# A mixture-of-experts stage: one branch for each whole product, with the folds inside the short way

## The chip, the cores and the metric

One core of a Trainium2 chip runs the whole program. The metric is the device time of one execution in microseconds (us), median of the runs. Engines are named as in the profile: PE is TensorE (matmul), PEld its weight loads, DVE is VectorE, ACT is ScalarE, POOL is GpSimd, SP issues DMAs.

## What is computed

Two layers of a hybrid decoder over 256 tokens of width 1024, in float32. The change touches only the channel mixer of the second layer, eight SwiGLU experts of which each token takes two:

```python
def moe_swiglu(x, w_router, w_gate, w_up, w_down):
    ...
    for e in range(N_EXPERTS):
        y = y + gates[:, e:e + 1] * swiglu(xt, w_gate[e], w_up[e], w_down[e])
    ...
# swiglu: (silu(x @ w_gate) * (x @ w_up)) @ w_down; 1024 -> 3584 -> 1024 for each expert
```

## The kernel before

Float32 products are made of three matmuls in a rounded format: each operand is split into a high part and a low rest, and hi·hi + hi·lo + lo·hi are added up (`mm3`, lines 161 to 164). A split of a weight tile (128 x 1024) is a cast on ScalarE (`whi`, line 152) and a subtraction on VectorE (`wlo`, line 153). Both kinds of tile have five buffers (`SPL`).

The tokens of an expert are gathered into up to 128 rows (`xg`, high and low side by side); 3584 is cut into seven pieces of 512, `m`. **A stage** is one pair (e, m). It makes gate(e, m), 4 splits; then `turn` transposes the hidden tile `hh` of the stage before into `ht` (four transposes, line 167, then ACT writes its high half, line 922, and DVE its low half, line 924); then up(e, m), 4 splits; then down of the stage before, 4 splits. So a stage has 12 splits, numbered here from 0: gate 0 to 3, up 4 to 7, down 8 to 11. Weights come in by chunks of two splits (1 MB) over SP's queue, some twelve chunks ahead.

**Two ways.** An expert with at most 64 tokens can do with two matmuls in place of three: the high and low rows of the tokens fill the 128 rows together, `x2`, and one matmul each by `whi` and `wlo` gives all four products (lines 877, 878; for down line 949, where the two rows of a token read the same weight). The results of the low rows then have to be added onto those of the high rows: ACT copies the accumulator (`fl`, line 850) and a matmul by a constant matrix adds it back shifted by a row, **the fold** (line 838). Whether an expert has so few tokens is known only at run time: `few[e]`, loaded in TensorE's register. `either` (line 826) puts the long way (`heavy`, 24 matmuls a product) and the short way (`light`, 16) behind a branch of TensorE's; `folded` puts the fold behind one of its own that is skipped in the long way. Expert 0 has no branch and takes the long way. Before the change each product has two `either` branches, of two splits each, and after the first of up and of down stands a `folded` branch, for gate and for up.

**Order of the work.** A planner in the compiler orders each engine's queue by what is ready, and a branch with its matmuls is one indivisible piece for it. `issue_after` ties keep some instructions behind others. What follows a split by a number of splits is put off by `defer(n, ...)`, run from `msplit`: the copy `fl` by 2, `silu` (line 894), the halves of `ht` and the multiplication `mult` (line 900) by 4.

Of the kernel before, what the change touches and what calls it, by code (L numbers as in the profile page):

```python
# [18 lines left out]
P = 128  # L19
# [68 lines left out]
def trunk(ctx: ExitStack, tc: tile.TileContext, x, consts, mconsts, vecs, lnrows, w_in, w_uq, w_ukv, w_o,  # L88
# [549 lines left out]
    def moe(pool, raws2, raws3, r, gb, rw):  # L638
# [196 lines left out]
        def folded(e, b, fl):  # L835
            if few[e] is not None:
                with tc.If(few[e] != 0):  # L837
                    nc.tensor.matmul(b, fold, fl[0], start=False, stop=True, skip_group_check=True)

        def gate_up(e, m, xg, part=None, mid=None):  # L840
# [3 lines left out]
            if part:  # L844
                part(0)

            def copy_for_fold(g, fl):
                with after(last[0]):
                    fl.append(pool.tile([P, 512], F32R, tag="fl", name="fl"))
                    nc.scalar.copy(fl[0], bs[g])  # L850

            fls = [[], []]
            for g, w in enumerate((e_gate, e_up)):
                raw = mchunk(w[e, m], 2 if g == 1 and (e, m) == LAST else 1)
                for q in range(2):
                    if part and g == 0:
                        sp = []
                        for k in range(4 * q, 4 * q + 4):
                            if k % 2 == 0:
                                if k < 6:  # L860
                                    part(k // 2 + 1)
                                sp.append(msplit(raw(k * 512, 1024)))
                            cs = slice((k % 2) * 512, (k % 2 + 1) * 512)
                            mm3(bs[g], xg[:, k, :, 0], xg[:, k, :, 1], sp[-1][0][:, cs], sp[-1][1][:, cs], k == 0, k == 7)
                        continue
                    sp = [msplit(raw(k * 512, 1024)) for k in (4 * q, 4 * q + 2)]
                    parts_ = [(k, sp[k // 2 % 2][0][:, k % 2 * 512:k % 2 * 512 + 512],
                               sp[k // 2 % 2][1][:, k % 2 * 512:k % 2 * 512 + 512]) for k in range(4 * q, 4 * q + 4)]

                    def heavy():  # L870
                        for k, hi, lo in parts_:
                            mm3(bs[g], xg[:, k, :, 0], xg[:, k, :, 1], hi, lo, k == 0, k == 7)

                    def light():
                        for k, hi, lo in parts_:
                            x2 = xg[:, k, 0:64, :].rearrange("p a b -> p (a b)")
                            nc.tensor.matmul(bs[g], x2, hi, start=(k == 0), stop=False)  # L877
                            nc.tensor.matmul(bs[g], x2, lo, start=False, stop=(k == 7))  # L878

                    either(e, heavy, light)  # L880
                    if g == 1 and q == 0:
                        folded(e, bs[0], fls[0])
                if dyn:
                    if g == 0 or (e, m) != LAST:
                        defer(FOLD_N, lambda g=g: copy_for_fold(g, fls[g]))
                    else:
                        copy_for_fold(g, fls[g])
                if g == 0:
                    if mid:
                        mid()  # L890

                    def silu():
                        with after(last[0]):
                            nc.scalar.activation(hh, bs[0], AF.Silu)  # L894

                    defer(SILU_N, silu)
# [5 lines left out]
            def fold_up():  # L902
                folded(e, bs[1], fls[1])
                if (e, m) == LAST:
                    mult()

            if e == 0 and m == 0:
                mult()
            elif (e, m) != LAST:
                defer(MULT_N, mult)  # L910
            return hh, fold_up
# [20 lines left out]
        def down(e, m, ht, yb, fold_up=None, hook=None):  # L932
            raw = mchunk(e_down[e, m], 2 if e == NE - 1 and m >= FM - 2 else 1)
            for q in range(2):
                sp = [msplit(raw(j * D, D)) for j in (2 * q, 2 * q + 1)]

                def heavy():
                    for j in (2 * q, 2 * q + 1):
                        hi, lo = sp[j % 2]
                        for n in range(2):  # L940
                            cs = slice(n * 512, n * 512 + 512)
                            mm3(yb[n], ht[:, j, 0], ht[:, j, 1], hi[:, cs], lo[:, cs], m == 0 and j == 0, m == FM - 1 and j == 3)

                def light():
                    for j in (2 * q, 2 * q + 1):
                        h2 = ht[:, j].rearrange("p a b -> p (a b)")[:, 0:256:2]
                        for n in range(2):
                            for i in range(2):
                                nc.tensor.matmul(yb[n], h2, sp[j % 2][i][:, n * 512:n * 512 + 512],  # L949
                                                 start=(m == 0 and j == 0 and i == 0), stop=(m == FM - 1 and j == 3 and i == 1))  # L950

                either(e, heavy, light)
                if q == 0 and fold_up:
# [111 lines left out]
        def finish(e, m, ht, fold_up=None, hook=None):  # L1065
# [3 lines left out]
            down(e, m, ht, yb[e], fold_up, hook)  # L1069
# [285 lines left out]
```

## Time and profile before

| | |
|---|---|
| median of 3 runs | 1475.29 us (1469.05 to 1476.32) |
| profiled execution, time | 1477.69 us |
| its span, first to last instruction | 1475.7 us |
| granted TensorE clock, mean | 0.981 |
| TensorE, VectorE, ScalarE busy | 94%, 82%, 70% |
| GpSimd busy | 5% |
| expert part | from about 488 us to 1450 us; with branches from about 605 us |

The page's busy shares are means over the whole span. A matmul row's duration overlaps with the next one, so the distance between starts is what a matmul takes in a row of them. An idle time in brackets names what the engine waited for; "PEq" is TensorE's sequencer and "issue" a wait that the profile can't name.

### The profile page before, as it was taken

To read this page: it belongs to the slowest core of one execution; us is meant where nothing else is said; L and a number is where in the kernel's file an instruction comes from. 1 tells how busy PE (TensorE), PEld (TensorE's weight loads), DVE (VectorE), ACT (ScalarE), POOL (GpSimd) and SP (SyncE) were. 2 spreads that over 40 slices of the span, in tenths; PEclk is the share of its full clock that TensorE was granted. 3 is DMA by queue.
4 is the path that set the end of the run, shared out by engine and by line. 5 is a ranking of instruction groups with operands and counts; after the bars stand their busy time and mean duration, and the time that the engine had idled before them with its cause. 6 is when DMAs were issued, how large, how long until landed. Compare 5 with 4: busy or idle time off the path is not lost. (4 is left out here: it accounts for less than half of the span.)

```text
span 1475.7 us, 20166 instructions
## 1 busy us (share of the span) xinstructions
PE 1379.9 (94%) x6927; PEld 1115.9 (76%) x6927; DVE 1204.0 (82%) x1590; ACT 1035.0 (70%) x1391; POOL 76.4 (5%) x113
## 2 busy tenths in 40 slices
PE   7999999999998999989889999998999999999995
PEld 6987999998986888766666677776677877777663
DVE  6577655547668799899999988899998888888997
ACT  3564444444655677878979877788887777778894
POOL 3112000003104000000000000000000000000001
PEclk8999999999998899999999999999999999999998
DMA  6733555544527599999999998989999898889980
GB/s 245 282 143 114 200 178 194 181 164 141 208 94 306 195 340 367 356 359 348 421 373 406 417 343 316 347 332 396 414 376 341 324 346 306 333 347 359 355 349 31
DMA packets 63526, 429.59 MB, mean 291 GB/s; under 512 B 7058, under 2 KB 7570, under 8 KB 15268
## 3 DMA queue, kind: packets, MB, share of 16 engines
q1 hardware_dynamic: 63364, 427.81, 75.9%
q8 instruction: 84, 1.38, 0.4%
q14 instruction: 46, 0.38, 0.1%
q0 software_dynamic: 32, 0.03, 0.0%
HBM read 426.76 MB, written 1.05 MB: 290 GB/s over the span
## 5 line engine op out<-in xcount | busy, mean ns | idle before, releaser
L153 DVE TENSOR_TENSOR wlo<-raw,whi 128x1024 fp32r<-128x1024 f32 (+3 forms) x801 | 933.7, 1213 | 156.7 <-ACT whi L152 155.1
L152 ACT CAST whi<-raw 128x1024 fp32r<-128x1024 f32 (+4 forms) x808 | 808.9, 1042 | 216.6 <-PE gu L586 44.0
L878 PE MATMUL eg<-wlo,xg 128*128 128x512 f32 x448 | 186.5, 416 | 1.8 <-DVE wlo L153 1.5
L162 PE MATMUL eg<-whi,xg 128*128 128x512 f32 x448 | 180.5, 403 | 6.8 <-PEq L837 6.8
L877 PE MATMUL eg<-whi,xg 128*128 128x512 f32 x448 | 180.3, 402 | 0.1
L163 PE MATMUL eg<-wlo,xg 128*128 128x512 f32 x448 | 176.9, 395 | 2.0 <-DVE wlo L153 1.7
L164 PE MATMUL eg<-whi,xg 128*128 128x512 f32 x448 | 176.0, 393 | 0.0
L878 PEld LDWEIGHTS eg<-wlo,xg 128*128 128x128 f32 x448 | 84.5, 189 | 50.1 <-DVE wlo L153 33.4
L162 PEld LDWEIGHTS eg<-whi,xg 128*128 128x128 f32 x448 | 87.3, 195 | 29.3 <-issue 12.8
L949 PE MATMUL y<-wlo,wk 128*128 128x512 f32 x224 | 96.7, 432 | 12.7 <-DVE wlo L153 12.6
L163 PEld LDWEIGHTS eg<-wlo,xg 128*128 128x128 f32 x448 | 87.4, 195 | 18.2 <-DVE wlo L153 3.8
L164 PEld LDWEIGHTS eg<-whi,xg 128*128 128x128 f32 x448 | 87.4, 195 | 16.0
L585 PE MATMUL gu<-xhi,whi 128*128 128x256 f32 x352 | 99.3, 282 | 0.1
L586 PE MATMUL gu<-xlo,whi 128*128 128x256 f32 x352 | 99.2, 282 | 0.2 <-DVE xlo L225 0.2
L587 PE MATMUL gu<-xhi,wlo 128*128 128x256 f32 x352 | 98.9, 281 | 0.0
L877 PEld LDWEIGHTS eg<-whi,xg 128*128 128x128 f32 x448 | 85.0, 190 | 15.9 <-issue 1.1
L949 PE MATMUL y<-whi,wk 128*128 128x512 f32 x224 | 93.3, 417 | 3.1 <-DVE wk L924 2.2
L162 PE MATMUL y<-whi,wk 128*128 128x512 f32 x224 | 90.2, 403 | 5.1 <-PEq L837 4.2
L163 PE MATMUL y<-wlo,wk 128*128 128x512 f32 x224 | 88.8, 396 | 1.6 <-DVE wlo L153 1.5
L164 PE MATMUL y<-whi,wk 128*128 128x512 f32 x224 | 88.5, 395 | 0.0
L949 PEld LDWEIGHTS y<-wlo,wk 128*128 128x128 f32 x224 | 45.1, 201 | 37.9 <-DVE wlo L153 31.7
L894 ACT ACTIVATE hh<-eg 128x512 f32<-128x512 f32 x56 | 33.6, 600 | 53.3 <-PEq L837 28.3
(307 smaller groups left out, 2147.3 us busy)
## 6 DMA issues: line engine op xcount, KB each, us to landing
raw<-in_e_gate SPq DMA_DIRECT2D x112, 1024.0 KB, 6.7
raw<-in_e_up SPq DMA_DIRECT2D x110, 1024.0 KB, 6.8
raw<-in_e_down SPq DMA_DIRECT2D x108, 1024.0 KB, 6.4
raw<-in_ffn_gu SPq DMA_DIRECT2D x22, 1024.0 KB, 4.9
raw<-in_ffn_dn SPq DMA_DIRECT2D x11, 1024.0 KB, 4.6
raw<-in_w_in SPq DMA_DIRECT2D x10, 960.0 KB, 4.6
raw<-in_w_o SPq DMA_DIRECT2D x8, 1024.0 KB, 6.2
gb<-in_lnrows SPq DMA_DIRECT2D x8, 512.0 KB, 4.3
```

The lines of the kernel that those rows point to most:

```text
L152: last[0] = nc.scalar.copy(hi[:, :n], src)
L153: last[1] = (eng or nc.vector).tensor_tensor(lo[:, :n], src, hi.bitcast(F32)[:, :n], ALU.subtract)
L162: nc.tensor.matmul(o, ahi, bhi, start=start, stop=False)
L163: nc.tensor.matmul(o, ahi, blo, start=False, stop=False)
L164: return nc.tensor.matmul(o, alo, bhi, start=False, stop=stop)
L585: nc.tensor.matmul(o, hi[:, cs], xhi[:, k, :], start=(g == 0 and k == 0), stop=False)
L586: nc.tensor.matmul(o, hi[:, cs], xlo[:, k, :], start=False, stop=False)
L587: nc.tensor.matmul(o, lo[:, cs], xhi[:, k, :], start=False, stop=(g == 1 and k == 7))
L877: nc.tensor.matmul(bs[g], x2, hi, start=(k == 0), stop=False)
L878: nc.tensor.matmul(bs[g], x2, lo, start=False, stop=(k == 7))
L894: nc.scalar.activation(hh, bs[0], AF.Silu)
L949: nc.tensor.matmul(yb[n], h2, sp[j % 2][i][:, n * 512:n * 512 + 512], start=(m == 0 and j == 0 and i == 0), stop=(m == FM - 1 and j == 3 a ...
```

## The change

Each of gate, up and down gets one branch over its four splits. The folds lose their own branches: gate's fold is a matmul in the short way of up, ahead of its seventh of eight k steps, and up's fold one in the short way of down, ahead of its last of four steps. Where down belongs to another expert than up (the first stage of an expert), up's fold keeps a branch of its own, after down. With branches, `silu` and `mult` are put off by one split more (5). In the very last pair, `mult` is called after down instead of with the fold. The splits of a product are all called ahead of its branch. Expert 0 keeps its order.

```diff
--- before.py
+++ after.py
@@ -832,10 +832,9 @@
             with cmp.Else():
                 light()
 
-        def folded(e, b, fl):
-            if few[e] is not None:
-                with tc.If(few[e] != 0):
-                    nc.tensor.matmul(b, fold, fl[0], start=False, stop=True, skip_group_check=True)
+        def fold_in(b, fl):
+            if fl:
+                nc.tensor.matmul(b, fold, fl[0], start=False, stop=True, skip_group_check=True)
 
         def gate_up(e, m, xg, part=None, mid=None):
             hh = hh_t()
@@ -843,48 +842,50 @@
             dyn = few[e] is not None
             if part:
                 part(0)
-
-            def copy_for_fold(g, fl):
+            fls = [[], []]
+
+            def copy_for_fold(g):
                 with after(last[0]):
-                    fl.append(pool.tile([P, 512], F32R, tag="fl", name="fl"))
-                    nc.scalar.copy(fl[0], bs[g])
-
-            fls = [[], []]
+                    fls[g].append(pool.tile([P, 512], F32R, tag="fl", name="fl"))
+                    nc.scalar.copy(fls[g][0], bs[g])
+
             for g, w in enumerate((e_gate, e_up)):
                 raw = mchunk(w[e, m], 2 if g == 1 and (e, m) == LAST else 1)
-                for q in range(2):
-                    if part and g == 0:
-                        sp = []
-                        for k in range(4 * q, 4 * q + 4):
-                            if k % 2 == 0:
-                                if k < 6:
-                                    part(k // 2 + 1)
-                                sp.append(msplit(raw(k * 512, 1024)))
-                            cs = slice((k % 2) * 512, (k % 2 + 1) * 512)
-                            mm3(bs[g], xg[:, k, :, 0], xg[:, k, :, 1], sp[-1][0][:, cs], sp[-1][1][:, cs], k == 0, k == 7)
-                        continue
-                    sp = [msplit(raw(k * 512, 1024)) for k in (4 * q, 4 * q + 2)]
-                    parts_ = [(k, sp[k // 2 % 2][0][:, k % 2 * 512:k % 2 * 512 + 512],
-                               sp[k // 2 % 2][1][:, k % 2 * 512:k % 2 * 512 + 512]) for k in range(4 * q, 4 * q + 4)]
-
-                    def heavy():
-                        for k, hi, lo in parts_:
-                            mm3(bs[g], xg[:, k, :, 0], xg[:, k, :, 1], hi, lo, k == 0, k == 7)
-
-                    def light():
-                        for k, hi, lo in parts_:
-                            x2 = xg[:, k, 0:64, :].rearrange("p a b -> p (a b)")
-                            nc.tensor.matmul(bs[g], x2, hi, start=(k == 0), stop=False)
-                            nc.tensor.matmul(bs[g], x2, lo, start=False, stop=(k == 7))
-
+                sp = []
+
+                def four(q):
+                    for k in (0, 2, 4, 6)[2 * q:2 * q + 2]:
+                        if part and g == 0 and k < 6:
+                            part(k // 2 + 1)
+                        sp.append(msplit(raw(k * 512, 1024)))
+
+                def heavy(ks=range(KD)):
+                    for k in ks:
+                        cs = slice(k % 2 * 512, k % 2 * 512 + 512)
+                        mm3(bs[g], xg[:, k, :, 0], xg[:, k, :, 1], sp[k // 2][0][:, cs], sp[k // 2][1][:, cs], k == 0, k == 7)
+
+                def light():
+                    for k in range(KD):
+                        if g == 1 and k == 6:
+                            fold_in(bs[0], fls[0])
+                        cs = slice(k % 2 * 512, k % 2 * 512 + 512)
+                        x2 = xg[:, k, 0:64, :].rearrange("p a b -> p (a b)")
+                        nc.tensor.matmul(bs[g], x2, sp[k // 2][0][:, cs], start=(k == 0), stop=False)
+                        nc.tensor.matmul(bs[g], x2, sp[k // 2][1][:, cs], start=False, stop=(k == 7))
+
+                if dyn:
+                    four(0)
+                    four(1)
                     either(e, heavy, light)
-                    if g == 1 and q == 0:
-                        folded(e, bs[0], fls[0])
+                else:
+                    for q in range(2):
+                        four(q)
+                        heavy(range(4 * q, 4 * q + 4))
                 if dyn:
                     if g == 0 or (e, m) != LAST:
-                        defer(FOLD_N, lambda g=g: copy_for_fold(g, fls[g]))
+                        defer(FOLD_N, lambda g=g: copy_for_fold(g))
                     else:
-                        copy_for_fold(g, fls[g])
+                        copy_for_fold(g)
                 if g == 0:
                     if mid:
                         mid()
@@ -893,22 +894,17 @@
                         with after(last[0]):
                             nc.scalar.activation(hh, bs[0], AF.Silu)
 
-                    defer(SILU_N, silu)
+                    defer(SILU_N + dyn, silu)
 
             def mult():
                 with after(dve[0]):
                     nc.vector.tensor_tensor(hh, bs[1], hh, ALU.mult)
 
-            def fold_up():
-                folded(e, bs[1], fls[1])
-                if (e, m) == LAST:
-                    mult()
-
             if e == 0 and m == 0:
                 mult()
             elif (e, m) != LAST:
-                defer(MULT_N, mult)
-            return hh, fold_up
+                defer(MULT_N + dyn, mult)
+            return hh, (lambda: fold_in(bs[1], fls[1])), mult
 
         def turn(hh, n, o=0):
             b = bank(acc, "ht")
@@ -929,28 +925,35 @@
                 halves()
             return ht
 
-        def down(e, m, ht, yb, fold_up=None, hook=None):
+        def down(e, m, ht, yb, fold_up=None, fe=None, hook=None):
             raw = mchunk(e_down[e, m], 2 if e == NE - 1 and m >= FM - 2 else 1)
-            for q in range(2):
-                sp = [msplit(raw(j * D, D)) for j in (2 * q, 2 * q + 1)]
-
-                def heavy():
-                    for j in (2 * q, 2 * q + 1):
-                        hi, lo = sp[j % 2]
-                        for n in range(2):
-                            cs = slice(n * 512, n * 512 + 512)
-                            mm3(yb[n], ht[:, j, 0], ht[:, j, 1], hi[:, cs], lo[:, cs], m == 0 and j == 0, m == FM - 1 and j == 3)
-
-                def light():
-                    for j in (2 * q, 2 * q + 1):
-                        h2 = ht[:, j].rearrange("p a b -> p (a b)")[:, 0:256:2]
-                        for n in range(2):
-                            for i in range(2):
-                                nc.tensor.matmul(yb[n], h2, sp[j % 2][i][:, n * 512:n * 512 + 512],
-                                                 start=(m == 0 and j == 0 and i == 0), stop=(m == FM - 1 and j == 3 and i == 1))
-
+            sp = []
+
+            def heavy(js=range(4)):
+                for j in js:
+                    for n in range(2):
+                        cs = slice(n * 512, n * 512 + 512)
+                        mm3(yb[n], ht[:, j, 0], ht[:, j, 1], sp[j][0][:, cs], sp[j][1][:, cs], m == 0 and j == 0, m == FM - 1 and j == 3)
+
+            def light():
+                for j in range(4):
+                    if j == 3 and fold_up and fe == e:
+                        fold_up()
+                    h2 = ht[:, j].rearrange("p a b -> p (a b)")[:, 0:256:2]
+                    for n in range(2):
+                        for i in range(2):
+                            nc.tensor.matmul(yb[n], h2, sp[j][i][:, n * 512:n * 512 + 512],
+                                             start=(m == 0 and j == 0 and i == 0), stop=(m == FM - 1 and j == 3 and i == 1))
+
+            if few[e] is not None:
+                sp.extend(msplit(raw(j * D, D)) for j in range(4))
                 either(e, heavy, light)
-                if q == 0 and fold_up:
+            else:
+                for q in range(2):
+                    sp.extend(msplit(raw(j * D, D)) for j in (2 * q, 2 * q + 1))
+                    heavy((2 * q, 2 * q + 1))
+            if fold_up and fe != e and few[fe] is not None:
+                with tc.If(few[fe] != 0):
                     fold_up()
             if hook:
                 hook()
...
```

## Rows read from the trace of the kernel before

**Rows 1.** The page, section 1: busy time, share of the span and instructions.

```profile
PE 1379.9 (94%) x6927; PEld 1115.9 (76%) x6927; DVE 1204.0 (82%) x1590; ACT 1035.0 (70%) x1391; POOL 76.4 (5%) x113
```

**Rows 2.** Stretches: length, busy us of PE, PEld, DVE, ACT, POOL; clock, DMA, GB/s.

```profile
520.60:589.20 68.60, 68.60 (x305) 57.01 (x305) 62.56 (x57) 53.95 (x56) 0.00 (x0) 1.00 0.92 352
1031.30:1076.00 44.70, 42.87 (x165) 27.46 (x164) 44.70 (x43) 40.42 (x50) 0.00 (x0) 1.00 1.01 416
1251.20:1343.10 91.90, 88.07 (x381) 70.27 (x380) 75.47 (x71) 70.35 (x81) 0.00 (x0) 1.00 0.89 341
```

**Rows 3.** The same table, seven stages each of experts 3 and 4.

```profile
832.80:966.50 133.70, 127.82 (x567) 102.56 (x566) 115.11 (x119) 102.85 (x125) 0.00 (x0) 1.00 0.90 342
966.50:1076.00 109.50, 101.82 (x413) 70.26 (x412) 107.29 (x109) 96.16 (x116) 0.00 (x0) 1.00 0.98 390
```

**Rows 4.** Timeline (start, duration us, what), PE, long way: over gate's second branch.

```profile
1194.03 0.39 PE L164 MATMUL eg<-whi,xg 128*128 128x512 f32 x1
1194.26 0.39 PE L162 MATMUL eg<-whi,xg 128*128 128x512 f32 x1
```

**Rows 5.** Timeline, PE, long way: over the branch of gate's fold.

```profile
1199.55 0.40 PE L164 MATMUL eg<-whi,xg 128*128 128x512 f32 x1
1200.26 0.50 PE L162 MATMUL eg<-whi,xg 128*128 128x512 f32 x1 [0.32 <-PEq L837]
1200.60 0.40 PE L163 MATMUL eg<-wlo,xg 128*128 128x512 f32 x1
```

**Rows 6.** Waits from 640 us on: total us, times, longest us.

```profile
ACT whi L152 <- PE eg L162: 29.2, 40, 1.4
...
PEld eg L162 <- issue: 12.8, 18, 0.8
...
PEld y L162 <- ACT whi L152: 10.1, 15, 0.8
```

**Rows 7.** Timeline, ACT and DVE, long way: silu and what stands behind it.

```profile
1200.08 0.60 ACT L894 ACTIVATE hh<-eg 128x512 f32<-128x512 f32 x1 [1.78 <-PEq L837]
...
1201.64 4.63 DVE L153 TENSOR_TENSOR wlo<-raw,whi 128x1024 fp32r<-128x1024 f32 x4 [2.62 <-ACT whi L152]
```

**Rows 8.** Timeline, DVE and PE, long way: mult, transposes, next gate.

```profile
1206.30 0.69 DVE L900 TENSOR_TENSOR hh<-eg,hh 128x512 f32<-128x512 f32 x1
...
1209.31 0.60 PE L167 MATMUL ht<-mc,hh 128*128 128x128 f32 x4
1209.66 0.48 PE L162 MATMUL eg<-whi,xg 128*128 128x512 f32 x1
```

**Rows 9.** Timeline, DVE, a whole short-way stage.

```profile
1030.32 9.16 DVE L153 TENSOR_TENSOR wlo<-raw,whi 128x1024 fp32r<-128x1024 f32 x8
1039.40 0.68 DVE L924 TENSOR_TENSOR wk<-ht,wk 128x512 fp32r<-128x512 f32 x1
1040.07 4.63 DVE L153 TENSOR_TENSOR wlo<-raw,whi 128x1024 fp32r<-128x1024 f32 x4
1044.62 0.68 DVE L900 TENSOR_TENSOR hh<-eg,hh 128x512 f32<-128x512 f32 x1
```

**Rows 10.** Timeline, ACT, the same stage; the first row ends with up's casts.

```profile
1030.26 5.79 ACT L152 CAST whi<-raw 128x1024 fp32r<-128x1024 f32 x6
1036.01 0.59 ACT L850 CAST fl<-eg 128x512 fp32r<-128x512 f32 x1
1036.49 0.59 ACT L922 CAST wk<-ht 128x512 fp32r<-128x512 f32 x1
1038.50 0.60 ACT L894 ACTIVATE hh<-eg 128x512 f32<-128x512 f32 x1 [1.42 <-PE eg L838]
1038.99 3.88 ACT L152 CAST whi<-raw 128x1024 fp32r<-128x1024 f32 x4
```

**Rows 11.** Timeline, PE, short way: from a split's wlo to the block's end.

```profile
1009.27 0.50 PE L878 MATMUL eg<-wlo,xg 128*128 128x512 f32 x1
...
1009.83 0.40 PE L878 MATMUL eg<-wlo,xg 128*128 128x512 f32 x1
```

More of the change, by code (lines that the diff above doesn't have):

```diff
@@ L1063, in moe, with finish @@
         ht = [None]
-        def finish(e, m, ht, fold_up=None, hook=None):
+        def finish(e, m, ht, fold_up=None, fe=None, hook=None):
             nonlocal post
@@ L1068, in finish @@
                 yb[e] = [bank(acc, "y") for _ in range(2)]
-            down(e, m, ht, yb[e], fold_up, hook)
+            down(e, m, ht, yb[e], fold_up, fe, hook)
             if m == FM - 1:
@@ L1087, in mid @@
                         ht[0] = turn(prev[2], HT_N)
-                hh, fold_up = gate_up(e, m, half[pr][1][e % 2], half[0][2] if e == 0 and m == 0 else None, mid)
+                hh, fold_up, mult = gate_up(e, m, half[pr][1][e % 2], half[0][2] if e == 0 and m == 0 else None, mid)
                 if e == 0 and m == 0:
@@ L1096, in moe, with hook @@
                     h2 = [ht[0]]
-                    finish(*prev[:2], ht[0], fold_up, (lambda: h2.append(turn(hh, 0, 1024))) if (e, m) == LAST else None)
+                    def hook():
+                        mult()
+                        h2.append(turn(hh, 0, 1024))
+                    finish(*prev[:2], ht[0], fold_up, e, hook if (e, m) == LAST else None)
                 if m == 3 and e == NE - 1:
```

## The prediction

> **What bounds the kernel now.** I read the page's first section, then a table of stretches of the expert part, then the timeline of one stage of each kind, then the waits. TensorE is busy 94% of the span [rows 1], but that is an average over two kinds of stage, and the change is only in the expert part (from about 605 us on, after expert 0).
>
> A stage is one (e, m): gate and up of this m, down of the m before. By the matmul counts [rows 2], a long-way stage has 76 matmuls (72 and 4 transposes; 305/4 and 381/5), a short-way stage about 54 (48, 2 folds, 4 transposes; 165/3). Three stretches [rows 2] give the lengths. Expert 0, which has no branches, takes 68.60/4 = 17.15 us a stage, with TensorE busy all the time. The same work behind branches takes 91.90/5 = 18.38 us; I use 18.3, since one of the five is longer. A short-way stage takes 44.70/3 = 14.90 us, and there VectorE is busy 44.70 of 44.70 us: its 12 subtractions, the low half of ht and the multiplication fill it without a hole [rows 9]. So: **long-way stages are bound by TensorE, and lose 1.15 us each to something that expert 0 does not have; short-way stages are bound by VectorE.** Of the 49 stages behind branches, 21 are long-way (experts 3, 5 and 6: 133.70 us for seven of them, against 109.50 us for seven short-way ones [rows 3], the rest of each being the scatter and gather stages).
>
> Where the 1.15 us lies is seen by following matmul starts in a long-way stage. Over a plain branch, between the two halves of gate, one matmul starts 0.23 us after the other, as anywhere [rows 4]: TensorE's queue holds work while its sequencer branches. Over the fold's branch, where the fold is not run, the next matmul starts 1200.26 - 1199.55 = 0.71 us after the last, and the one after that 0.34 us later [rows 5]: 0.71 + 0.34 - 2 x 0.23 = **0.59 us**. The row names TensorE's sequencer at L837: where there is no fold, what stands in its place counts for it only once the matmuls before it have ended. Two such places a stage, 1.18 us, are the whole difference to expert 0. The waits say the same for the expert part: 12.8 and 10.1 us before weight loads, 18 and 15 times [rows 6].
>
> **The change, part by part.**
>
> *Branches of gate, up and down.* Six a stage become three, over 49 stages 294 become 147. Removed at no gain in long-way stages: 0.23 us over the branch [rows 4]. In short-way stages TensorE waits for VectorE anyway.
> [...]
>
> *Fold branches.* 14 an expert become one (in the first stage, where down belongs to the expert before). In long-way stages 3 x 13 = 39 places of 0.59 us go: **-23.0 us**. That is the main term. Against expert 0 it is 21 x 1.15 = 24 us for all 42 places, less 3 x 0.59: -22.4. Bounds: a place gives no less than its queue wait, 0.32 [rows 5] (-12.5), and no more than 0.71 + 0.34 with no matmul counted (-41, which cannot be, since 17.15 is the floor).
>
> *The folds in the short way.* The same 56 matmuls, at 0.23 us, now before the last quarter of up and of down. TensorE has room there (42.87 us busy of 44.70 by modelled ends, and it waits at each new wlo). Cost 0; what it would cost without that cover is what the fold's matmul takes now.
>
> *What waits for the folds.* silu moves from the fourth cast after gate to the fifth, mult from the last cast of down to the first of the next gate. No DMA moves: SP still issues a chunk when VectorE has read the old one, in the same order, and POOL has no work here. Behind silu on ScalarE stand the casts of down, behind those VectorE's subtractions, behind those TensorE. Behind mult on VectorE stand the next subtractions, and the transposes wait for it. A reader behind a branch must wait for as much of the way taken as covers the other way: before, silu in long-way stages waits 1.78 us for the place of a fold that is not run, and VectorE then has 2.62 us without a cast [rows 7], and still TensorE lacks nothing (no hole beyond the 0.59). The fold stands 13th of the short way's 17 matmuls, so in the long way I put its place about four matmuls before the end (the tails of the two ways counted alike), 0.92 us before TensorE goes on. mult takes 0.69 us [rows 8] and the last matmul's own 0.39 us runs on: 0.39 + 0.69 + two handovers of 0.05 = 1.18, against 0.92 + 0.23 = 1.15 to the next slot. Cost about 0.03, and the restart behind the transposes [rows 8] is in expert 0's stage too. For a handover that comes late, with the slow first step of 0.34 [rows 5], I take **+0.1 us** a long-way stage, 21 x 0.1 = **+2.1 us**. Bounds: 0, if mult is out in time; 0.94 if it is held to the end of the long way (rival 2).
>
> *Longer blocks and five buffers.* A block now holds four of the five whi and wlo buffers. In the long way a block uses a split in 6 x 0.23 = 1.38 us, VectorE makes one in 1.135 (9.08/8, from [rows 9]), so after a block starts the queue catches up. Casts wait for TensorE in long-way stages already (29.2 us, 40 times [rows 6]), at no loss. If buffers are freed some four matmuls later than now, that is 0.9 us of 18. Cost 0 in long-way stages; bound 0.5 (a subtraction that comes late for down's second split).
>
> *Where the fold's copy stands on ScalarE.* This decides the short-way stages. The code calls for gate's copy two splits after gate, yet in the trace it stands behind the fourth [rows 10]: the planner lets casts through until the copy's block has ended. Then silu waits 1.42 us for the fold and the next cast ends (1038.99 + 1.05 = 1040.04) just as VectorE is free for it at 1040.07 [rows 9, 10]. After the change the copy's block is the whole gate, which gives buffers back as it goes, so I expect casts 5 to 7 (counted from 0 through the stage) ahead of it again, and 9 to 11 ahead of silu. Then nothing is late for VectorE, whose work is unchanged: **0 us** in 28 short-way stages. If the copy stands where the code calls it, behind cast 5, ScalarE is held: gate's last wlo, then 0.05 + (1009.83 + 0.40 - 1009.27 = 0.96) [rows 11] + 0.04 to the copy, 0.48 for it (1036.49 - 1036.01 [rows 10]), cast 1.05, 0.04: 2.62 us until VectorE can start split 6, against 2 x 1.135 - 0.08 = 2.19 us of work in hand. That is 0.43 us a stage, **12 us** in all (rival 1). Transfers: no ScalarE or VectorE row waits for a weight chunk, and long-way stages at 17.25 us ask for less than the 416 GB/s that short-way ones draw [rows 2].
>
> *Sum.* -23.0 + 2.1 + 0 = -21 us. The profiled execution took 1477.69 us (span 1475.66 and 2.0 around it), so 1456.7; the median of the three runs shown is 2.4 us lower than that execution, so **1454.5 us** for the median.
>
> **Rivals.**
> 1. *The copy of gate is not let back, silu is.* 28 x 0.43 = +12; long-way stages 0.35 worse (mult and the casts of down come late by 0.28 and 0.1), +7: -21 + 19, about 1473, within 0.5%. For it: the code's own order. Against: [rows 10].
> 2. *mult is held to the end of the long way.* 0.94 instead of 0.1 us in 21 stages: +18, about 1472. For it: in the trace a reader of a skipped fold waits for the whole branch to be over [rows 7]. Against: there the fold was a block of its own.
> 3. **Slower:** *silu goes ahead of the casts of down.* Both its fold and the copy then hold ScalarE. Long way: the cast of down's second split starts only after silu, 0.60 + 1.05 + 1.22 us after a fold place 1.15 us before up's end, against 1.15 + 1.38 + 0.23 us of TensorE's work; with the up copy (0.48) before the next cast, some 0.8 us a stage, +17. Short way: 0.43 and again about 0.2 us behind silu, 28 x 0.65 = +18. Together -21 + 35: about 1489. It decides once the short-way stages lose over 21/28 = 0.75 us each, or both kinds lose as here. For it: silu stands ahead of down's first cast now [rows 10].
> 4. *The branches were not covered.* If each of the 63 branches that go in long-way stages (3 in 21) gave the 0.32 us for which TensorE waits on its sequencer [rows 5], 20 us more would go: about 1434. Against: [rows 4].
> [...]
>
> **How the numbers follow.** Forecast 1454.5 with 0.60 (1450 to 1463 by its own terms: 24 us without a cost, or 0.4 us more a long-way stage); rivals 1 and 2 together 0.21; rival 3 0.14; rival 4 0.05. The range leaves out rival 3, takes in rivals 1 and 2 and goes half way to rival 4: 1444 to 1478. About 0.5% (7 us) is what a measurement of this kernel can tell from no change. Faster: 0.60 + 0.05 + 0.04 of rivals 1 and 2 = 0.69. Same: 0.17. Slower: 0.14.
>
> **What would show it.** Long-way stages of 17.2 to 17.3 us, matmul starts 0.23 us apart through a whole stage; L837's waits gone but for one place an expert. The copy behind the fourth cast of up; short-way stages still 14.9 us with VectorE full. Wrong if VectorE waits for casts in short-way stages (rivals 1, 3), or transposes wait for mult by more than 0.3 us in long-way ones (rival 2). What would make it wrong outright is ScalarE's order, which the trace of before cannot show for the new blocks.

## The result, and the profile after

The changed kernel takes **1554.87 us** (median of 4 runs, 1552.98 to 1558.95) against 1472.24 us for the kernel before (4 runs, one more than stood in the table of before): a ratio of 1.0563, 95% interval 1.0523 to 1.0603. It is slower by 5.6%, where 1454.5 was forecast in a range that ended at 1478. The profiled execution took 1554.44 us, has a span of 1552.5 us against 1475.7 and a mean granted clock of 0.959 against 0.981.

The stretches come first (columns as in [rows 2]): the seven stages of expert 3 and of expert 4, between them the stage in which expert 3 gathers the tokens of the next pair, then one short-way and one long-way stage.

```profile
856.10:1003.60 147.50, 129.69 (x565) 105.56 (x564) 112.84 (x117) 99.43 (x122) 0.00 (x0) 0.97 0.81 300
915.40:947.50 32.10, 22.26 (x109) 18.37 (x108) 18.95 (x27) 16.05 (x24) 0.00 (x0) 0.95 0.59 218
1003.60:1125.00 121.40, 99.65 (x413) 77.61 (x412) 110.49 (x111) 96.84 (x116) 0.00 (x0) 0.94 0.95 365
1059.70:1076.40 16.70, 13.81 (x57) 10.95 (x55) 15.26 (x15) 13.60 (x16) 0.00 (x0) 0.90 0.96 368
1354.50:1372.70 18.20, 17.33 (x80) 14.18 (x78) 15.21 (x15) 13.74 (x16) 0.00 (x0) 1.00 0.92 332
```

Against [rows 3], experts 3 and 4 are longer by 13.8 and 11.9 us. A short-way stage went from 14.90 to 16.70 us (five of them to 15.2), a long-way one from 18.3 to 18.2, and VectorE is no longer full in the short way. The waits from 640 us on say what came in (in this kernel mult is L901, the matmuls of gate and up are L873 and L874 in the short way and L163 among others in the long way, the gather's copies are L748 and L750):

```profile
PE ht L167 <- DVE hh L901: 98.8, 42, 5.2
ACT whi L152 <- PE eg L873: 68.2, 48, 4.3
ACT whi L152 <- PE eg L163: 65.3, 19, 5.9
ACT xg L750 <- DVE xg L748: 45.1, 12, 7.3
DVE xg L748 <- PE gx L742: 38.1, 12, 7.0
```

Before, the transposes' wait was this:

```profile
PE ht L167 <- DVE hh L900: 14.9, 12, 1.7
```

The "issue" waits of the folds' places [rows 6] are gone, as meant. In their place the transposes wait for mult, 98.8 us in all instead of 14.9; casts wait for TensorE to give buffers back; and the gather's copies, which had held ScalarE and VectorE for 2.9 and 1.4 us at most (13.4 and 9.2 us in all), hold them for up to 7 us at a time.

The stages differ in what they lost. By the distances from one mult to the next in the two traces, the 19 plain short-way stages (all but the first two of an expert and those with a gather) lost 22 us together, the 13 plain long-way ones gained 1, the three with a gather lost 34 and the first two stages of the experts, with the scatter, 25. So most of the loss doesn't lie in plain stages.

**A short-way stage, on VectorE** (start, duration, what, idle time before it), to be read beside [rows 9]:

```profile
1061.96 1.23 DVE L153 TENSOR_TENSOR wlo<-raw,whi 128x1024 fp32r<-128x1024 f32 x1 [0.50 <-ACT whi L152]
1063.67 1.23 DVE L153 TENSOR_TENSOR wlo<-raw,whi 128x1024 fp32r<-128x1024 f32 x1 [0.48 <-ACT whi L152]
1065.14 1.23 DVE L153 TENSOR_TENSOR wlo<-raw,whi 128x1024 fp32r<-128x1024 f32 x1 [0.25 <-ACT whi L152]
1066.29 0.68 DVE L920 TENSOR_TENSOR wk<-ht,wk 128x512 fp32r<-128x512 f32 x1
1067.06 8.26 DVE L153 TENSOR_TENSOR wlo<-raw,whi 128x1024 fp32r<-128x1024 f32 x7
1075.23 0.68 DVE L901 TENSOR_TENSOR hh<-eg,hh 128x512 f32<-128x512 f32 x1
```

The seven subtractions behind `wk` are the four of down and **three of the next gate**: mult stands behind split 2 of the next gate. The code asks for a place behind split 0. The same stage on TensorE:

```profile
1071.75 0.40 PE L837 MATMUL eg<-fl,fold 128*128 128x512 f32 x1
...
1072.68 0.40 PE L945 MATMUL y<-wlo,wk 128*128 128x512 f32 x1
1075.97 0.66 PE L167 MATMUL ht<-mc,hh 128*128 128x128 f32 x4 [2.89 <-DVE hh L901]
...
1077.49 0.63 PE L873 MATMUL eg<-whi,xg 128*128 128x512 f32 x1
1077.92 0.63 PE L874 MATMUL eg<-wlo,xg 128*128 128x512 f32 x1
```

The fold is out at 1072.15, and mult starts 3.1 us later, so TensorE, which has finished down, idles 2.89 us at the transposes. Behind that its matmuls follow 0.43 us apart instead of 0.23, and the table of stretches shows why. The rows are the gate of this stage, behind an idle time of the same kind; the rest of the stage; the idle time of 2.89 us; and the next gate:

```profile
1059.60:1063.60 4.00, 4.00 (x13) 3.18 (x12) 3.09 (x3) 2.06 (x2) 0.00 (x0) 0.58 1.02 406
1063.70:1072.70 9.00, 9.00 (x41) 7.37 (x39) 8.53 (x8) 8.64 (x12) 0.00 (x0) 1.00 0.93 351
1072.70:1076.00 3.30, 0.41 (x3) 0.03 (x1) 3.30 (x5) 2.87 (x4) 0.00 (x0) 1.00 0.96 365
1076.40:1080.30 3.90, 3.90 (x14) 3.11 (x12) 3.22 (x4) 2.09 (x2) 0.00 (x0) 0.61 1.01 426
```

Through the idle time the granted clock is 1.00, and in the 3.9 us behind it 0.61, as it was 0.58 in the gate before. In the second of these gates it is 0.94 from 1076.40 to 1077.40 us, 0.50 from there to 1080.40, and 1.00 from 1080.80 on, with TensorE busy all along. Between the two gates it is back at 1.00. About half of a gate's 16 matmuls start 0.43 us apart instead of 0.23, its buffers come back late, casts 5 to 7 start late, and that is what VectorE's 0.50, 0.48 and 0.25 us at the head of the stage are.

**A long-way stage** loses its time at the same wait, without a fall of the clock (1.00 in the stage, and 1.00 in the 2.7 us behind the hole):

```profile
1371.01 0.40 PE L164 MATMUL y<-whi,wk 128*128 128x512 f32 x1
1372.28 0.66 PE L167 MATMUL ht<-mc,hh 128*128 128x128 f32 x4 [0.87 <-DVE hh L901]
```

```profile
1369.26 2.36 DVE L153 TENSOR_TENSOR wlo<-raw,whi 128x1024 fp32r<-128x1024 f32 x2 [0.50 <-ACT whi L152]
1371.54 0.68 DVE L901 TENSOR_TENSOR hh<-eg,hh 128x512 f32<-128x512 f32 x1
```

Matmuls follow 0.23 us apart through the whole stage, the holes of [rows 5] are gone, and then one hole of 1371.01 to 1372.28 us, 1.27 instead of 0.23, gives nearly all of it back: 1.04 of 1.18 us.

**The stage with the gather** (expert 3, 915.4 to 947.5 us) took 32.1 us, against 21.3 before:

```profile
890.30:911.60 21.30, 20.83 (x107) 17.36 (x105) 18.03 (x22) 15.90 (x23) 0.00 (x0) 1.00 0.79 297
```

In the changed kernel, on TensorE, VectorE and ScalarE:

```profile
915.17 0.36 PE L742 MATMUL gx<-pm,xth 128*128 128x256 f32 x1
...
920.91 0.52 PE L742 MATMUL gx<-pm,xth 128*128 128x256 f32 x3
921.46 0.42 DVE L748 CAST xg<-gx 128x256 fp32r<-128x256 f32 x1 [4.49 <-PE gx L742]
921.92 0.39 ACT L750 CAST xg<-gx 128x256 fp32r<-128x256 f32 x1 [6.95 <-DVE xg L748]
```

Between the first and the second row lie the 24 matmuls of gate's one block. The gather's next three matmuls can't stand inside it. Meanwhile the copies that need them are already at the head of VectorE's and ScalarE's queues, so no split is made for 4.5 and 7 us. Before, the gather's matmuls stood between the two halves of gate as well.

### The profile page after: what moved, and what is told of

Read it like the earlier page. It is cut to its first block, busy times and chain, and to the rows that moved or that the text cites. A ratio compares the mean times of both kernels' runs of the same rounds, so it can differ in the third digit from the quotient of the medians.

```text
span 1552.5 us, 19779 instructions
## 1 busy us (share of the span) xinstructions
PE 1376.3 (89%) x6927; PEld 1150.5 (74%) x6927; DVE 1208.0 (78%) x1590; ACT 1026.6 (66%) x1391; POOL 77.9 (5%) x113
## 5 line engine op out<-in xcount | busy, mean ns | idle before, releaser
L874 PE MATMUL eg<-wlo,xg 128*128 128x512 f32 x448 | 192.5, 430 | 4.8 <-DVE wlo L153 4.8
L873 PE MATMUL eg<-whi,xg 128*128 128x512 f32 x448 | 195.2, 436 | 0.6 <-ACT wk L918 0.6
L163 PE MATMUL eg<-wlo,xg 128*128 128x512 f32 x448 | 179.3, 400 | 4.5 <-DVE wlo L153 4.5
L162 PE MATMUL eg<-whi,xg 128*128 128x512 f32 x448 | 181.8, 406 | 0.0
L164 PE MATMUL eg<-whi,xg 128*128 128x512 f32 x448 | 178.4, 398 | 0.0
L167 PE MATMUL ht<-mc,hh 128*128 128x128 f32 x224 | 39.7, 305 | 98.8 <-DVE hh L901 98.8
L874 PEld LDWEIGHTS eg<-wlo,xg 128*128 128x128 f32 x448 | 93.7, 209 | 30.6 <-DVE wlo L153 8.7
L167 PEld LDWEIGHTS ht<-mc,hh 128*128 128x128 f32 x224 | 26.6, 150 | 117.8 <-DVE hh L901 100.2
L873 PEld LDWEIGHTS eg<-whi,xg 128*128 128x128 f32 x448 | 94.2, 210 | 22.5 <-ACT wk L918 1.0
L163 PEld LDWEIGHTS eg<-wlo,xg 128*128 128x128 f32 x448 | 89.2, 199 | 21.0 <-DVE wlo L153 5.4
L164 PEld LDWEIGHTS eg<-whi,xg 128*128 128x128 f32 x448 | 89.0, 199 | 16.9
L162 PEld LDWEIGHTS eg<-whi,xg 128*128 128x128 f32 x448 | 89.4, 200 | 15.7
L585 PE MATMUL gu<-xhi,whi 128*128 128x256 f32 x352 | 98.8, 281 | 0.1
L945 PE MATMUL y<-wlo,wk 128*128 128x512 f32 x224 | 89.8, 401 | 2.9 <-DVE wlo L153 2.9
L945 PE MATMUL y<-whi,wk 128*128 128x512 f32 x224 | 89.4, 399 | 2.7 <-DVE wk L920 1.5
L164 PE MATMUL y<-whi,wk 128*128 128x512 f32 x224 | 89.2, 398 | 0.0
L163 PE MATMUL y<-wlo,wk 128*128 128x512 f32 x224 | 89.1, 398 | 0.0
L162 PE MATMUL y<-whi,wk 128*128 128x512 f32 x224 | 88.7, 399 | 0.3 <-ACT hh L895 0.3
```

The costliest lines, as they stand in the source:

```text
L162: nc.tensor.matmul(o, ahi, bhi, start=start, stop=False)
L163: nc.tensor.matmul(o, ahi, blo, start=False, stop=False)
L164: return nc.tensor.matmul(o, alo, bhi, start=False, stop=stop)
L167: nc.tensor.transpose(o, src, ident)
L585: nc.tensor.matmul(o, hi[:, cs], xhi[:, k, :], start=(g == 0 and k == 0), stop=False)
L873: nc.tensor.matmul(bs[g], x2, sp[k // 2][0][:, cs], start=(k == 0), stop=False)
```

## The experiments

Two theories were made from this profile. **M**: plain stages lose their time to the place of mult, in the short way through TensorE's clock as well (**C**). **G**: stages into which other work has to be fitted lose it because a block of a whole product can't be interrupted. Rival **B**: a whole product as one block, against five buffers, is what costs; rival **F**: the folds inside the blocks cost. The runs:

| run | median us | ratio to before, 95% interval |
|---|---|---|
| the changed kernel | 1554.87 | 1.0563 (1.0523 to 1.0603) |
| mult_early | 1481.89 | 1.0039 (1.0021 to 1.0057) |
| warm | 1535.0 | 1.0392 (1.0370 to 1.0413) |
| halves_g3 | 1521.78 | 1.0295 (1.0278 to 1.0312) |
| halves_all | 1459.41 | 0.9883 (0.9867 to 0.9900) |
| hold_g3 | 1459.54 | 0.9888 (0.9871 to 0.9904) |
| halves_all_hold | 1449.6 | 0.9834 (0.9815 to 0.9853) |
| hold_g3_m0 | 1461.74 | 0.9908 (0.9891 to 0.9924) |
| hold_g3_m1 | 1450.63 | 0.9822 (0.9806 to 0.9839) |
| hold_g3_m01 | 1446.2 | 0.9800 (0.9784 to 0.9816) |

The part of the program ahead of the experts is the same in all of these kernels and took 496 to 503 us in their traces, so a difference of a few us between two runs says little.

### mult_early: mult behind one subtraction of the next gate

```diff
-            last[1] = (eng or nc.vector).tensor_tensor(lo[:, :n], src, ...)
+            with after(*held):
+                last[1] = (eng or nc.vector).tensor_tensor(lo[:, :n], src, ...)
...
-                    nc.vector.tensor_tensor(hh, bs[1], hh, ALU.mult)
+                    mi = nc.vector.tensor_tensor(hh, bs[1], hh, ALU.mult)
+                if dyn:
+                    held[:] = [mi]
```

> The changed kernel with one edit: the subtractions of the next gate behind the first may not be issued ahead of the multiplication, so that mult stands behind one subtraction of the next gate on VectorE (the place for which the code asks) and not behind three. Theory M (the lost time of plain stages is the place of mult): in short-way stages the transposes wait under 1 us for mult instead of 2.9, TensorE's clock does not fall behind them, a stage takes 15.0 to 15.4 us instead of 16.72; in long-way stages the wait of 0.87 us goes nearly whole, 17.3 us instead of 18.17; 28 x 1.4 + 21 x 0.85 = 57 us less, about 1497. Rival B (a whole product as one block, against five buffers, sets the stage): the wait moves to casts that lack a buffer, the stages keep their length, 1545 to 1560.

Measured: 1481.89, 73 us less than the changed kernel, by a tie in the order of VectorE's queue alone. Stretches: a short-way stage, a long-way stage, the gather's stage of expert 3.

```profile
1035.10:1049.90 14.80, 13.56 (x57) 9.17 (x56) 14.80 (x15) 13.51 (x16) 0.00 (x0) 1.00 1.01 416
1295.30:1312.50 17.20, 17.20 (x80) 14.17 (x77) 15.12 (x15) 13.75 (x17) 0.00 (x0) 1.00 0.96 369
884.70:915.30 30.60, 23.97 (x105) 19.67 (x104) 18.18 (x27) 14.83 (x24) 0.00 (x0) 0.89 0.59 221
```

Short-way stages are at 14.8 with VectorE full again, long-way ones at 17.2 with TensorE full: blocks of whole products and folds inside them cost a plain stage nothing, so B and F fall there. The gain is larger than expected (73 against 57), but only in part from where it was expected: by the distances from one mult to the next the plain short-way stages gave 30 us, the plain long-way ones 14, the experts' first two stages 17 and the gathers' stages 9; 4 lie ahead of the experts, where nothing differs. How near the edge mult is in the long way shows in its timeline (VectorE, then TensorE; mult is L903 here, the transposes L169):

```profile
1308.30 1.23 DVE L155 TENSOR_TENSOR wlo<-raw,whi 128x1024 fp32r<-128x1024 f32 x1 [0.31 <-ACT whi L153]
1311.29 0.69 DVE L903 TENSOR_TENSOR hh<-eg,hh 128x512 f32<-128x512 f32 x1 [1.77 <-PE y L165]
```

```profile
1310.86 0.39 PE L165 MATMUL y<-wlo,wk 128*128 128x512 f32 x1
...
1312.04 0.66 PE L169 MATMUL ht<-mc,hh 128*128 128x128 f32 x4
```

VectorE now waits 1.77 us for the skipped fold's place, which is the end (1310.86 + 0.39) of the fifth matmul from down's end, the one with four behind it. The transposes start 0.24 us behind the last matmul at 1311.80, with no hole.

### warm: the clock by itself

```diff
+                    if few[e] is not None and prev[0] == e and (e, m) != LAST:
+                        with tc.If(few[e] != 0):
+                            for _ in range(12):
+                                nc.tensor.matmul(yb[e][0][0:64], fo[:, :, 1], half[pr][1][e % 2][...],
+                                                 start=False, stop=False, skip_group_check=True)
```

> The changed kernel, order unchanged, plus twelve matmuls with a zero stationary (they add nothing to y) between down's short way and the transposes, where TensorE idles 2.9 us, in stages behind branches except the first of an expert and the last; the long way skips them. Theory C (a part of the loss is TensorE's clock: behind the idle time gate's matmuls follow 0.43 us apart instead of 0.23, so that buffers come back late for casts 5 to 7): with TensorE busy the granted clock stays at its upper level, gate's matmuls follow at 0.23, VectorE's three waits of 0.50, 0.48 and 0.25 us shrink by 0.8 to 1.2 us in all, a short-way stage falls to 15.5 to 15.9 us: 24 x 1.0 = 24 us less, about 1530. Rival (the clock costs nothing, the wait for mult is all): 1550 to 1565, with short-way stages at 16.7 us or longer.

Measured: 1535.0, 20 us less for 12 matmuls more a stage. A short-way stage by the table of stretches, and the filler on TensorE's timeline:

```profile
1051.60:1066.80 15.20, 15.04 (x70) 11.47 (x67) 14.94 (x15) 13.41 (x16) 0.00 (x0) 1.00 1.00 407
```

```profile
1063.29 2.92 PE L1109 MATMUL y<-xg,fold 128*64 128x512 f32 x12
1066.36 0.66 PE L167 MATMUL ht<-mc,hh 128*128 128x128 f32 x4 [0.16 <-DVE hh L901]
```

mult is as late as in the changed kernel, and yet the stage takes 15.20 instead of 16.70, with a granted clock of 1.00 in its gate too (1051.80 to 1055.70 us). So of the 1.9 us that a short-way stage lost against 14.8, **1.5 are the clock**, and only 0.4 the late mult itself: TensorE has room for 2.9 us of idle time in a stage bound by VectorE, but not for a gate half of whose matmuls start 0.43 us apart instead of 0.23. The filler stands in 23 stages, one fewer than the expectation counted, and the gain is under 23 x 1.5 = 34.5 us since five of them had kept the clock in the changed kernel (15.2 us from one mult to the next, where the others took 16.6 or more), and experts 3 and 5, with nothing to gain, took 2.3 and 1.3 us more.

### halves_g3: only the gathers' stages in halves

```diff
+def in_halves(e, m):
+    return e in (1, 3, 5) and m == 3
...
-                if dyn:
+                if dyn and not in_halves(e, m):
                     four(0)
                     four(1)
                     either(e, heavy, light)
                 else:
                     for q in range(2):
                         four(q)
-                        heavy(range(4 * q, 4 * q + 4))
+                        ks = range(4 * q, 4 * q + 4)
+                        either(e, lambda: heavy(ks), lambda: light(ks))
```

(and so in `down`.)

> The changed kernel, but gate, up and down of the three stages in which the tokens of the next two experts are gathered (experts 1, 3 and 5, m = 3) run as two blocks each again, as before the change; folds stay in the short way. Theory G (steps of the gather can only stand between blocks, and hold VectorE and ScalarE for a whole block): these stages took 28.4, 32.2 and 35.3 us and fall to about 18, 21.5 and 21.5; some 30 us less, about 1525. Rival: the gather is slow for another reason (the order around it as the fold moved), then these stages keep 30 us and more, and the time stays within 5 us of 1555.

Measured: 1521.78, 33 us less, from three of 49 stages. Expert 3's:

```profile
905.40:929.10 23.70, 21.83 (x114) 18.51 (x112) 18.57 (x24) 17.77 (x25) 0.00 (x0) 1.00 0.80 287
```

It went from 32.1 to 23.7 us and expert 5's from 35.3 to 23.9. Gate starts ahead of the transposes there, so the stretch takes in a part of the stage before; from one mult to the next they went from 31.9 to 21.4 and from 35.1 to 21.3, as expected. G holds; the rival falls.

### halves_all: only the folds moved

The predicate above returns True for all stages: two branches a product everywhere, as before the change.

> One half of the change alone: two branches for each product, as before, but the folds stand in the short way's blocks (in the second block of up and of down), with silu and mult asked for one split later, as in the change. mult then stands behind two subtractions of the next gate. Theories M and G: the gathers are back at 21 us, long-way stages lose their fold places and take 17.2 to 17.5 us, short-way stages pay for mult's place in part, 15.0 to 15.6 us: 1450 to 1475. Rival F (it is the folds inside the blocks that cost, since silu and mult wait longer): short-way stages stay at 16.5 us or more, and only the gathers and the long way gain: about 1505.

Measured: 1459.41, faster than before by 1.2%. A long-way and a short-way stage:

```profile
1235.90:1253.00 17.10, 17.10 (x79) 14.20 (x77) 15.81 (x15) 14.04 (x17) 0.00 (x0) 1.00 0.98 376
1019.80:1034.60 14.80, 14.21 (x55) 9.10 (x54) 14.80 (x15) 13.73 (x17) 0.00 (x0) 1.00 1.01 417
```

Long-way stages take 17.1 to 17.2 us and short-way ones 14.8, better than the 15.0 to 15.6 expected: with half blocks mult behind two subtractions makes the transposes of a plain stage wait for 0.8 us at most, and the clock stays at 1.00 in these two stages. F falls in full.

### hold_g3, halves_all_hold, hold_g3_m0, hold_g3_m1, hold_g3_m01: both mends, and what is left

These combine the two edits above and change only which stages run in halves: the three gathers' stages; all; the gathers' and each expert's first (m = 0); the gathers' and each second (m = 1); the gathers' and both.

> Both mends of the changed kernel together: mult behind one subtraction of the next gate, and the three gather stages in two blocks a product; all other stages keep one branch for the whole of a product. Theories M and G say that the two are apart and add up: against the run with mult early alone (1481.9) the three gather stages (25.2, 30.6 and 29.6 us there) fall to about 18, 21.5 and 21.5, together 24 us: 1455 to 1462. Rival: they share a cause (the gather was slow because mult was late behind it), then the second mend adds less than 10 us: 1472 or more.

> Two branches for each product everywhere, folds in the short way's second blocks, and mult behind one subtraction of the next gate. It differs from the run with both mends only in the number of branches (two a product instead of one in 46 of 49 stages). Theory: a branch over which TensorE's queue holds work costs nothing, so the two are within 4 us of each other, and within 4 us of 1459 (mult behind two subtractions already cost nothing in the halves). [...]

Measured: 1459.54 and 1449.6. The second mend adds 22 us, as expected, so the gathers' loss doesn't come from the late mult alone. But the two don't simply add up: without the tie the halves of the gathers' stages gave 33 us. Some 10 us of what these stages lost is given back by either mend (the tie alone gave 9 there). The second comparison missed: halves everywhere were not within 4 us of the run with both mends, but 10 us faster. Plain stages are equal in both kernels (14.82 and 17.16 us from one mult to the next), so **the number of branches is worth nothing there either way**; the kernels differ at an expert's start: its second stage, in which the expert before is scattered, is shorter by 11 us in all with halves, and the stages beside it longer by 3. Against halves_all, in which mult stands behind two subtractions, the tie gave 10 us (1459.4 to 1449.6; 7 by the ratios), and by the traces at the experts' starts too: there mult's place costs something with halves as well, against the expectation.

> As the run with both mends, but the first stage of each expert behind branches runs in halves too. In the changed kernel the first stage of a short-way expert behind a long-way one took 17.1 us against 14.7 before. Theory: the whole block of gate in such a stage waits for what the halves let through earlier; halves give back about 2 us in two or three of seven such stages: 3 to 6 us less than the run with both mends. Rival (the first stages only shift their boundary): no difference beyond 2 us.

> The run with both mends (1459.5), but the second stage of each expert, in which the expert before is scattered and its pair's weights are prepared, runs in halves too. By the distances from one multiplication to the next, the run with halves everywhere (1449.6) differs from the one with both mends only here: 24.4, 22.2, 22.8, 25.0 and 20.9 us against 20.5, 20.7, 20.5, 23.5 and 18.7 in experts 3 to 7, 11 us in all, while plain stages are equal at 14.8 and 17.2. Theory G2 (a step of the scatter too can only stand between blocks): about 1450. Rival (the loss arises in the first stage, whose gate waits behind the down of the expert before): within 3 us of 1459.

> The run with both mends, with the first and the second stage of each expert in halves. Theory G2: as with the second stage alone, within 3 us of 1450. Rival (the first stage only gives its part back when both are in halves): this one 1450, the one with the second stage alone 1455 or more.

Measured: 1461.74, 1450.63 and 1446.2. The first stage alone gives nothing (2 us more: that expectation was wrong), the second alone gives the 9 us, as G2 said, and both together the best median of the case, 2.0% under the kernel before. Whether the first stage helps beside the second stays open: the intervals of those two overlap. Expert 3's second stage in the run with the gathers' alone, and the scatter's additions in it on VectorE:

```profile
845.70:868.40 22.70, 20.82 (x88) 16.72 (x86) 17.11 (x20) 14.16 (x17) 0.00 (x0) 0.92 0.82 317
851.65 2.48 DVE L991 TENSOR_TENSOR r<-r,sc 128x512 f32<-128x512 f32 x4 [3.43 <-PE sc L986]
```

The same in the best one:

```profile
838.20:859.20 21.00, 19.76 (x90) 16.00 (x89) 19.11 (x21) 15.90 (x20) 0.00 (x0) 1.00 0.90 344
845.78 0.69 DVE L991 TENSOR_TENSOR r<-r,sc 128x512 f32<-128x512 f32 x1 [1.17 <-PE sc L986]
```

The scatter's later matmuls stand behind the whole of gate's block, from 851.21 us on, and VectorE waits 3.43 us for them; with halves most of them stand between the two (840.99 to 842.13 us) and the wait is 1.17. Behind the longer wait TensorE lacks a `wlo` for 1.88 us, and its granted clock falls here too (0.92 over the stage).

## Why the prediction was wrong

- **What bounds the stages** held: 17.2 us of TensorE and 14.8 us of VectorE are the floors in every kernel in which nothing else is late.
- **Branches of gate, up and down at no gain** held: plain stages with one and with two branches a product take the same time (14.82 and 17.16 us from one mult to the next, in hold_g3 and in halves_all_hold). What [rows 4] show is the distance of 0.23 us over a branch; that TensorE's queue holds work meanwhile is the forecast's reading of it. The longer ways brought no hole: TensorE is busy for 17.20 of 17.20 us of a long-way stage with whole blocks (mult_early) and for 17.10 of 17.10 with halves (halves_all). Rival 4 fell.
- **Fold places, -23.0 us**, held in mechanism and size: the waits on them went, and a long-way stage falls from 18.3 to 17.2 once nothing takes their place (mult_early, halves_all). In the changed kernel itself the gain was eaten, 18.2.
- **Folds at no cost in the short way** held: VectorE stays full at 14.8 us in mult_early.
- **ScalarE's order**, called the point that decides, came out as forecast (1065.49 is gate's copy, behind the last cast of up; 1069.76 is silu, behind the last cast of down; the row of four casts lies between):

```profile
1065.49 0.59 ACT L850 CAST fl<-eg 128x512 fp32r<-128x512 f32 x1
1065.97 3.90 ACT L152 CAST whi<-raw 128x1024 fp32r<-128x1024 f32 x4
1069.76 0.61 ACT L895 ACTIVATE hh<-eg 128x512 f32<-128x512 f32 x1
```

  Rivals 1 and 3 fell with it. The kernel was slower, as rival 3 had it, but not through its mechanism. Their sign, VectorE waiting for casts in the short way, did come (1.2 us in the stage shown), through the buffers that a slow gate gave back late.
- **The step that failed is mult's place on VectorE.** The forecast read it from the code ("the first of the next gate") and priced the handover at 0.1 us in the long way, nothing in the short way. It cost 1.04 us in the long way (a hole of 1.27 us instead of 0.23) and 1.8 in most short-way stages (16.7 us instead of 14.9), the next bullet's part included. For ScalarE's copy it had noticed from [rows 10] that the planner puts a reader of a block behind whatever can be issued before the block's end; the same reasoning on VectorE, with mult as the reader of a fold that now lies inside down's block, puts further subtractions ahead of it. That the planner counts the fold as done only with its block is argued from the order; the order itself, three subtractions instead of one, and its price, 73 us in all, 44 of them in plain stages, are shown. The time at which mult *could* run, four matmuls before down's end, was forecast rightly and is the 1.77 us wait above. Rival 2 asked whether that time comes too late; it doesn't. Its sign (transposes that wait over 0.3 us for mult in the long way) did come, and its price of 0.94 us a long-way stage is near the 1.04 measured, but by luck: mult wasn't held by the end of the long way but stood behind two subtractions too many.
- **A term that was missing: TensorE's clock.** In the trace of before the stretches of [rows 2] and [rows 3] run at 1.00; the forecast took an idle TensorE in a stage bound by VectorE to cost nothing ("TensorE waits for VectorE anyway"). It cost 1.5 us in most short-way stages (16.70 against 15.20 in warm), by the granted clock behind it (0.61 in the gate shown, 1.00 in warm).
- **A second term that was mis-sized: the longer blocks**, "cost 0, bound 0.5", which were priced for buffers only. Stages with a gather or a scatter were left to "the rest" of [rows 3]. With mult early the gathers cost 22 us (1481.9 to 1459.5) and the first two stages of the experts 13 (1459.5 to 1446.2; 9 of them lie there by the traces), because steps that stood between the halves of a product had to wait for a whole one. Most of the kernel's loss lay in these stages, 34 and 25 us against before, not in the plain ones that the forecast added up.

In this order of mends the account from 1554.9 to the best kernel's 1446.2 is 73 + 22 + 13 us; in another order the first two divide otherwise (33 + 62). What remains is 2.0% under the kernel before; the forecast's terms came to 1.4%.

## What to carry over

When a small operation comes to depend on something inside a branch, read its new place from the order of the engine that runs it, and count the work put ahead of it, instead of reading it from the number that the code passes. A block that can't be interrupted is cheap in a plain stage and dear in each stage into which other work must be fitted; look for those stages first and leave the blocks short there. An engine with room to idle may still be slowed by the idling, as TensorE was behind most holes of 2.8 to 3.0 us in the short way here (a granted clock down to 0.50): check the granted clock behind each new hole.

## What was not expected of the hardware

The clock falls in most, not all, of the short-way stages of the changed kernel. One stage later the same idle time leaves it alone:

```profile
1089.30:1092.70 3.40, 0.56 (x4) 0.13 (x3) 3.40 (x5) 2.93 (x4) 0.00 (x0) 1.00 0.96 354
1093.00:1096.50 3.50, 3.50 (x18) 2.87 (x17) 3.23 (x4) 2.47 (x3) 0.00 (x0) 1.00 1.01 405
```

That stage took 15.20 us from one mult to the next and its neighbours 16.66 and 16.76, with the same order and the same wait. In all, the clock fell behind 18 of the 23 holes of 2.8 to 3.0 us in the short way: it was 0.72 to 0.73 in the 6 us behind each of these, and 1.00 behind the other five. So the price of such a hole is not the same each time, and what decides it was not settled. And matmuls that add nothing to the result made the kernel 20 us faster.
